# Where the last head pair's combine is traced in a hybrid decoder trunk

## The chip, the cores and the metric

The kernel runs on one core of a Trainium2 chip. The metric is the device time of one execution in microseconds (us), the median of several runs. TensorE (PE) multiplies matrices and turns blocks by multiplying with the identity; VectorE (DVE), ScalarE (ACT) and GpSimd (POOL) do elementwise work; SyncE (SP) issues the transfers between HBM and SBUF. Each engine works through its own queue in order, and semaphores tie the queues together.

## The reference

A decoder trunk of two layers over 1024 tokens of 1024 features, float32. Layer 0 has a mixer of two halves side by side; layer 1 has gated linear attention; both end in a gated feed-forward network. What matters here is layer 0's mixer, cut:

```python
def even_mixer(h, w_in, ..., w_out):
    z = h @ w_in
    u, v, q, k, vb = jnp.split(z, ...)
    a_out = chunked_gmlp(gelu(u), gelu(v), a_ln_g, a_ln_b, a_ws, a_bs)   # u * (mix of layer-normed v)
    ...
    for window, dilation in B_BRANCHES:            # ((128, 1), (512, 4), (2048, 16))
        o_r, l_r = dilated_branch(qh, kh, vh, window, dilation)
    wts = jax.nn.softmax(jnp.stack(lses), axis=0)
    o = jnp.einsum('rbhs,rbhsc->bhsc', wts, jnp.stack(outs))
    ...
    return jnp.concatenate([a_out, b_out], axis=-1) @ w_out
```

So the output projection reads, for each token, 512 features of the gMLP half (`a_out`) and 512 of the attention half (`b_out`), and `b_out` is a weighted sum of branches whose weights come from the branches' maxima and denominators.

## The kernel before, in words

Activations stand in `hq`, turned (features on partitions) and split into a high and a low fp32r part; a product is three matmuls, high by high, high by low and low by high (`PASSES`). The sequence is cut into 8 tiles of 128 tokens. One tile of a projection to 512 columns (`mm_tok`, line 190) is 8 feature blocks by 3 matmuls, 24 in all. Weights arrive raw in one of 4 buffers (`load_raw`, line 110) and are split by ACT (line 100, or 105 with a gain) and DVE (line 101, or 106) into one of `NW = 8` buffers (`wp`).

**Layer 0's mixer.** `attention` goes through four pairs of heads. `project(p)` computes q, k and v of a pair and the branch of dilation 1 into the tiles `ot{p}n0` and `ot{p}n1` (512 tokens each, with two columns for the maxima and two for the denominators); `dilated(p)` computes the other two branches together in the order of the residues and writes them to `od` in HBM (line 750). The loads `on` (line 788) bring them back in token order, in two halves `g`. `combine` and `combined` then join `ot` and `on` of half `g`: on DVE a minimum (`cM`, line 759), two subtractions (762), on ACT an `Exp` (763), on DVE two products (770), a sum (771), a reciprocal (772) and a product (773); then POOL scales the 128x512 of `ot` and DVE those of `on` (both line 776), DVE adds them (778), and SP writes the sum to `bcat[g]` (779), 128 of whose 512 columns belong to the pair.

For pairs 0 to 2 the combine is called from the next pair's `project`, behind its tiles 3 and 4 (`then`). The last pair has no next one. While its dilated branches run, `gmlp` projects v, and after each half of four tiles mixes the 8 groups (`pm`, line 605) and puts the result into `mx` (DVE, line 606). `u_proj` projects u: for each tile ACT takes the gelu (`ut`, line 616) and DVE multiplies it into `mx` (line 617). In its `consume`, behind one of the tiles, it calls `last()`, which does the last pair's combine for both halves (lines 804 to 806).

**Layer 0's output projection** (`out_first`, line 432). `prep(n)` loads `cat` (line 1122: 512 features of tile n from `bcat[n // 4]`) and `xh` (line 438), turns four blocks of `mx` and four of `cat` on PE (`pc`, line 442), and splits the result into `hq`. `AHEAD = 1`: tile 0 is prepared before the weights `wo` are split, each later tile one ahead. `out_half` multiplies (`po`, line 190), adds into `xh` (429) and writes it out (430). At tile 2 `first_sides` begins (the loads `qg`, line 219). The weights `wo` take the buffers that `wu`, the weights of u, leave. The second half's weights (`wo10r` to `wo13r`) are loaded into the raw buffers that the first half's leave.

**What sets the order.** The code is traced in program order; a planner then simulates the engines and transfers and lays each queue out anew, by program order among what it takes to be ready. `tc.keep_in_program_order` ties an instruction behind the one traced before it on its engine. The minimum `cM` is tied so; for the last pair the instruction before it is the multiply of the tile at which `last()` is called (line 617), and for the second half the last subtraction of the first. All else in the combine is placed by its data. [...] The buffers of `gv` and `ut` are the same two.

## Time and profile before

| | us |
|---|---|
| median of 3 runs | 2196.88 |
| lowest and highest | 2193.66, 2197.9 |
| the profiled execution | 2195.83 |
| its span, first to last instruction | 2194.0 |

The mean granted TensorE clock of the profiled execution is 0.994. Its span is 1.83 us shorter than its time. In what follows, a row of a timeline gives the start in us from the span's beginning, the duration in us, the engine, the line, the operation, written tile `<-` read tiles, shapes and how many instructions are merged in the row; brackets at its end give the idle time of the engine before it and what ended it. SPq is the queue of transfers issued by SyncE; a transfer's row lasts as long as its issue. The mixer of layer 0 lies in the first 400 us, the u projection between 331 and 394 us, and layer 0's output projection behind it.

### The profile page before, as it was taken

What the parts mean: (1) busy time and instruction counts of PE and PEld (TensorE: products, weight loads), DVE (VectorE), ACT (ScalarE), POOL (GpSimd) and SP (SyncE); (2) the same over time, 40 slices, a digit from 0 to 9 for tenths busy, and PEclk for the clock granted to TensorE, in tenths of its full rate; (3) what the DMA queues carried; (4) which work ended last, traced back from release to release, by engine and by line L of the source; (5) the groups of instructions that cost most, each with busy time, mean ns of one, the idle gap of its engine ahead of it and who ended that gap; (6) DMA issues with size and microseconds to landing.
All of it is one profiled execution on the core that took longest, in us unless ns stands there. A gap on an engine that the chain in (4) does not pass through costs nothing.

```text
span 2194.0 us, 29873 instructions
## 1 busy us (share of the span) xinstructions
PE 2147.0 (98%) x10508; PEld 1816.2 (83%) x10508; DVE 1533.2 (70%) x2459; ACT 1042.7 (48%) x2006; POOL 489.0 (22%) x519
## 2 busy tenths in 40 slices
PE   8999999899999999999999999999999999999999
PEld 8999987687888888878889788878788888888887
DVE  5566653567888788855577777667787878885554
ACT  6555664245444444444454455534544444454443
POOL 4444410003334342200010011110232424320000
PEclk9999999899999999999999999999999999999999
DMA  4122212565544444585563123377544454457555
GB/s 148 47 72 81 78 35 59 179 247 189 163 158 158 154 154 159 187 291 179 204 236 113 68 97 104 104 258 265 194 145 153 158 165 157 168 176 268 204 195 203
DMA packets 157254, 349.59 MB, mean 159 GB/s; under 512 B 17408, under 2 KB 54272, under 8 KB 156720
## 3 DMA queue, kind: packets, MB, share of 16 engines
q1 hardware_dynamic: 157104, 347.68, 46.9%
q8 instruction: 83, 1.36, 0.3%
q14 instruction: 67, 0.55, 0.1%
HBM read 239.02 MB, written 108.59 MB: 158 GB/s over the span
## 4 chain that ended last, share of the span: by engine, by line
PE 88%; DVE 4%; DMA 3%; ACT 3%; issue 1%; POOL 1%; SPq 0%; ACTq 0%; DVEq 0%
PE puB L290 11%; PE pgB L290 11%; PE po L190 7%; PE pj L190 6%; PE pgC L290 5%; PE puC L290 5%; PE pv L190 5%; PE pdB L397 5%; PE pdC L397 5%; PE pdO L397 4%; PE puA L290 3%; PE pgA L290 2%; PE pdP L397 2%; PE pdQ L397 2%; PE pBq L972 2%; PE pu L190 2%
## 5 line engine op out<-in xcount | busy, mean ns | idle before, releaser
L101 DVE TENSOR_TENSOR da<-ar,da 128x512 fp32r<-128x512 f32 x154 | 106.3, 690 | 156.2 <-ACT da L100 156.0
L100 ACT CAST da<-ar 128x512 fp32r<-128x512 f32 x154 | 95.9, 623 | 209.4 <-PE pdC L397 90.7
L190 PE MATMUL po<-wo,hq 128*128 128x512 f32 x768 | 186.4, 397 | 0.6 <-DVE hq L101 0.3
L190 PEld LDWEIGHTS po<-wo,hq 128*128 128x128 f32 x768 | 142.5, 189 | 30.2 <-DVE hq L101 1.4
L190 PE MATMUL pj<-wq,hq 128*128 128x384 f32 x768 | 157.8, 352 | 2.3 <-ACT vN L701 1.3
L190 PE MATMUL pv<-wv,hq 128*128 128x512 f32 (+2 forms) x768 | 141.1, 340 | 2.4 <-DVE b L1004 1.6
L190 PEld LDWEIGHTS pj<-wq,hq 128*128 128x128 f32 x768 | 135.3, 195 | 4.0 <-ACT vN L701 2.1
L397 PE MATMUL pdB<-dw,da 128*128 128x512 f32 x528 | 136.2, 391 | 0.9 <-ACT dw L100 0.9
L397 PE MATMUL pdC<-dw,da 128*128 128x512 f32 x528 | 135.8, 390 | 0.0
L190 PEld LDWEIGHTS pv<-wv,hq 128*128 128x128 f32 x768 | 118.7, 189 | 17.6 <-DVE b L1004 2.1
L397 PEld LDWEIGHTS pdB<-dw,da 128*128 128x128 f32 x528 | 98.7, 188 | 22.2 <-ACT dw L100 1.3
L397 PEld LDWEIGHTS pdC<-dw,da 128*128 128x128 f32 x528 | 99.0, 188 | 20.5
L256 POOL TENSOR_TENSOR S1g<-rg 128x512 f32<-128x512 f32 x20 | 29.3, 1464 | 384.2 <-DMA wsd<-D 325.0
L101 DVE TENSOR_TENSOR dw<-wr,dw 128x512 fp32r<-128x512 f32 x154 | 105.8, 687 | 10.7 <-ACT dw L100 10.4
L140 POOL TENSOR_SCALAR rn<-ssq 128x1 f32<-128x1 f32 x24 | 9.5, 397 | 461.3 <-ACT h L148 245.3
L397 PE MATMUL pdO<-dw,da 128*128 128x512 f32 x396 | 102.2, 389 | 0.2 <-DVE dw L101 0.2
L100 ACT CAST dw<-wr 128x512 fp32r<-128x512 f32 x154 | 95.0, 617 | 15.3 <-DMA wr<-in_w_dn 7.0
L397 PEld LDWEIGHTS pdO<-dw,da 128*128 128x128 f32 x396 | 74.3, 188 | 16.0 <-DVE dw L101 0.6
L319 DVE SCALAR_TENSOR_TENSOR t<-g,cw,t 128x1022 f32<-128x1022 f32 x44 | 75.6, 1719 | 0.1
L318 DVE SCALAR_TENSOR_TENSOR t<-g,cw,t 128x1023 f32<-128x1023 f32 x44 | 58.3, 1325 | 16.4 <-ACT t L317 16.4
L303 DVE TENSOR_TENSOR g<-g,s1g 128x512 f32<-128x512 f32 x22 | 16.2, 737 | 73.9 <-ACT s1g L302 73.9
L320 ACT ACTIVATE t<-t 128x1024 f32<-128x1024 f32 x44 | 46.7, 1061 | 29.8 <-DVE t L319 29.6
(1070 smaller groups left out, 5405.9 us busy)
## 6 DMA issues: line engine op xcount, KB each, us to landing
ar<-actd SPq DMA_DIRECT2D x70, 512.0 KB, 3.5
rd<-in_w_down SPq DMA_DIRECT2D x44, 512.0 KB, 3.6
wsd<-D SPq DMA_DIRECT2D x88, 256.0 KB, 2.6
rg<-in_w_gate SPq DMA_DIRECT2D x42, 512.0 KB, 3.6
ru<-in_w_up SPq DMA_DIRECT2D x42, 512.0 KB, 4.6
wr<-wsd SPq DMA_DIRECT2D x40, 512.0 KB, 4.5
actd<-t SPq DMA_DIRECT2D x66, 256.0 KB, 2.1
wr<-in_w_dn SPq DMA_DIRECT2D x30, 512.0 KB, 5.0
```

Source lines behind the costliest of these rows:

```text
L100: (hi or A.copy)(dst[0], src)
L101: (lo or V.tensor_sub)(dst[1], src, f32(dst[0]))
L140: G.tensor_scalar(r, ssq, 1.0 / n, EPS, op0=ALU.mult, op1=ALU.add)
L190: T.matmul(o, L[i], R[jj][:, sl], start=(k == 0 and (ii, jj) == PASSES[0]), stop=(k == nk - 1 and (ii, jj) == PASSES[-1]))
L256: G.tensor_tensor(sums[name], x, y, op=op)
L290: T.matmul(o, L[ii][:, j * P : j * P + P], right[p][:, jj, j, :], skip_group_check=more, start=(not more and j == 0 and (ii, jj) == PASSES ...
L303: V.tensor_add(C22, C22, s1)
L318: V.scalar_tensor_tensor(t[:, 1:], g[:, : S - 1], w(1), t[:, 1:], op0=ALU.mult, op1=ALU.add)
L319: V.scalar_tensor_tensor(t[:, 2:], g[:, : S - 2], w(0), t[:, 2:], op0=ALU.mult, op1=ALU.add)
L320: A.activation(t, t, AF.Silu)
L397: T.matmul(o, L[ii][:, t * P : t * P + P], R[jj], skip_group_check=more, start=start and not more and (ii, jj) == PASSES[0], stop=stop and ...
L972: T.matmul(o, L[ii][:, j * P : j * P + P], right[p][:, jj, j, :], skip_group_check=more, start=(not more and j == 0 and (ii, jj) == PASSES ...
```

## The change

In `u_proj`, `last()` is called behind the tile with index 1 instead of that with index 4. The functions that it calls are unchanged.

```diff
             A.activation(t, pj, AF.Gelu, scale=r0[:, n : n + 1])
             V.tensor_mul(mixed[n], mixed[n], t)
-            if n == 4:
+            if n == 1:
                 last()
```

What `last()` calls:

```python
def last():
    for rest in [weights(g) for g in range(2)]:   # weights(g): combine(p, g, [os[g], ons[g]])
        rest()
```

Both minima, with their subtractions and `Exp`, are traced first, then both halves of the rest.

## The prediction

> **What bounds the kernel now.** The page comes first: its span and its busy shares.

> ```profile
> span 2194.0 us, 29873 instructions
> ...
> PE 2147.0 (98%) x10508; PEld 1816.2 (83%) x10508; DVE 1533.2 (70%) x2459; ACT 1042.7 (48%) x2006; POOL 489.0 (22%) x519
> ```

> TensorE is busy for all but 47 us of the span, so an edit that takes no matmul away can gain only from those 47 us, or from matmuls that run slower than they could. The view of waits, for PE alone, says where the 47 us lie (total, times, longest):

> ```profile
> PE pc L442 <- DMA cat<-bcat: 9.3, 1, 9.3
> PE pt L529 <- DMA x<-in_x: 5.4, 2, 4.6
> ...
> PE puB L290 <- ACT s1u L302: 1.4, 2, 0.7
> ```

> The longest single wait of the whole kernel is for `cat<-bcat`, the load of what the combine of the last pair writes. The second is the start of the program, and then come waits of about one us. The tail of the u projection, from the timeline of all engines (start, duration, engine, line, tiles):

> ```profile
> 386.53 0.16 DVE L759 TENSOR_TENSOR cM<-ot3n,on 128x8 f32<-128x8 f32 x1
> ...
> 391.29 1.37 POOL L776 TENSOR_TENSOR ot3n<-ot3n,cE 128x512 f32<-128x512 f32 x1 [1.01 <-DVE cE L773]
> 391.67 1.53 DVE L778 TENSOR_TENSOR ot3n<-ot3n,on 128x512 f32<-128x512 f32 x1
> ...
> 393.23 0.36 SPq L779 DMA_DIRECT2D bcat<-ot3n  x1
> ...
> 393.56 0.60 PE L442 MATMUL pc<-ident,mx 128*128 128x128 f32 x4
> ...
> 394.10 0.69 ACT L616 ACTIVATE ut<-pu,r 128x512 f32<-128x512 f32 x1
> ...
> 394.68 0.61 ACT L100 CAST wo<-wo03r 128x512 fp32r<-128x512 f32 x1
> ...
> 396.14 0.68 DVE L778 TENSOR_TENSOR ot3n<-ot3n,on 128x512 f32<-128x512 f32 x1
> 396.74 0.68 DVE L101 TENSOR_TENSOR wo<-wo02r,wo 128x512 fp32r<-128x512 f32 x1
> 396.85 0.38 SPq L779 DMA_DIRECT2D bcat<-ot3n  x1
> ...
> 397.45 0.33 SPq L110 DMA_DIRECT2D wo12r<-in_ev_w_out  x1
> 397.82 0.47 SPq L1122 DMA_DIRECT2D cat<-bcat  x1
> ...
> 403.41 1.12 PE L442 MATMUL pc<-ident,cat 128*128 128x128 f32 x4 [9.25 <-DMA cat<-bcat]
> 404.14 1.07 ACT L100 CAST hq<-pc 128x512 fp32r<-128x512 f32 x2 [8.85 <-PE pc L442]
> ...
> 404.75 1.29 DVE L101 TENSOR_TENSOR hq<-pc,hq 128x512 fp32r<-128x512 f32 x2 [5.53 <-ACT hq L100]
> 404.77 1.22 PE L190 MATMUL po<-wo,hq 128*128 128x512 f32 x2 [0.25 <-ACT hq L100]
> ```

> The combine begins at 386.53 and its second add ends at 396.82, while PE has its last u matmul behind it at 393.56. PE turns the four `mx` blocks that it can and then stands for 9.25 us. The load it waits for was issued at 397.82, behind a weight load on the same queue, and took 5.6 us. The price is not the wait alone. The windows view (PE, PEld, DVE, ACT, POOL busy; granted clock; DMA share; GB/s) shows the clock around it:

> ```profile
> 394.20:398.00 3.80, 0.00 (x0) 0.00 (x0) 3.80 (x8) 1.09 (x2) 0.00 (x0) 0.75 0.96 261
> 398.00:403.40 5.40, 0.00 (x0) 0.00 (x0) 1.23 (x3) 0.00 (x0) 0.00 (x0) 0.50 0.97 308
> ...
> 409.00:410.00 1.00, 1.00 (x4) 0.76 (x4) 0.36 (x1) 0.59 (x1) 0.00 (x0) 0.61 0.33 115
> 410.00:411.00 1.00, 1.00 (x6) 0.82 (x5) 0.33 (x1) 0.00 (x0) 0.00 (x0) 1.00 0.85 207
> ```

> During the wait the granted clock falls to 0.50 and comes back only inside the slice 409 to 410, so the first tile of the output projection is computed at half speed. How long a tile should take is read from the starts of the transposes that open each tile's period:

> ```profile
> 413.61 0.38 PE L442 MATMUL pc<-ident,mx 128*128 128x128 f32 x2
> ...
> 420.46 0.38 PE L442 MATMUL pc<-ident,mx 128*128 128x128 f32 x2
> ...
> 426.85 0.38 PE L442 MATMUL pc<-ident,mx 128*128 128x128 f32 x2
> ```

> From 420.46 to 426.85, 6.39 us, PE does 24 `po` matmuls and 8 transposes. From 404.77 to 413.61 it does the same in 8.84 us: 2.45 us are lost to the clock.

> **The change part by part.** It takes nothing away and adds nothing. `last()` is traced after tile 1 instead of tile 4, so the pin of `cM` (L759) ties it behind the multiply of tile 1 rather than tile 4. Moved are, for two halves: 16 small DVE operations, four large DVE ones, two POOL multiplies, two `Exp` on ACT and two `bcat` writes on SP. Where they arrive, the timeline shows:

> ```profile
> 362.39 1.52 SPq L788 DMA_DIRECT2D on<-od  x2
> ...
> 367.42 1.29 DVE L617 TENSOR_TENSOR mx<-mx,ut 128x512 f32<-128x512 f32 x2
> 368.20 1.29 ACT L616 ACTIVATE ut<-pu,r 128x512 f32<-128x512 f32 x2 [8.36 <-DVE mx L617]
> 368.94 4.59 PE L190 MATMUL pu<-wu,hq 128*128 128x512 f32 x19 [0.88 <-ACT ut L616]
> ...
> 374.00 0.92 DVE L606 TENSOR_SCALAR mx<-pm,bs 128x256 f32<-128x256 f32 x2 [3.30 <-PE pm L605]
> ...
> 375.59 0.69 ACT L616 ACTIVATE ut<-pu,r 128x512 f32<-128x512 f32 x1 [6.09 <-PE pu L190]
> ...
> 378.81 1.03 PE L605 MATMUL pm<-mx,ws 128*128 128x256 f32 x4
> ...
> 382.67 1.28 ACT L763 ACT_TABLE_LOAD   x1
> ```

> The landing of `on`, from the view of that tile in this stretch, and the stretch as one window:

> ```profile
> DMA to landing us min/median/max: 3.1/3.3/3.5
> ```

> ```profile
> 368.90:386.00 17.10, 17.06 (x75) 14.20 (x76) 4.63 (x11) 3.26 (x4) 0.00 (x0) 1.00 0.00 0
> ```

> *Does it wait at its new place?* Tile 1 is projected early, but its multiply runs only at the end of the pair at 367.42, by 368.7, because it needs the first half of `mx`. The two `on` loads are issued at 362.39 and by 363.9 and take at most 3.5 us: landed by 367.4. The new wait of `cM` is 0 (bounds 0 and 1 us). Queued behind it on DVE would be the second half's evacuations (L606) and the multiplies of tiles 2 and 3.

> *DVE.* 16 small operations at 0.16 us, two multiplies and an add at 0.68, the slow add at 1.53: 2.6 + 2.0 + 1.5 = 6.1 us. In the window DVE is idle for 17.1 - 4.63 = 12.5 us, so it fits. If the whole 6.1 us stood in one block ahead of the pair at 374.00, that would end at about 376 to 377, and the next group mixing on PE, `pm` at 378.81, still finds its banks free: 0. If the block also pushes the pair that stands at 368.6, `pm` at 373 is held for up to 2 us. I take 0.

> *ACT.* Two table loads of 1.28 us and two short `Exp` go from the place at 382 to 389 to one behind the two gelus at 368.20, where ACT then sits idle for 6.09 us. Cost 0; if the planner puts them between those two gelus, the second is late by about 3 us, but PE has the 4.6 us of tile 4's matmuls at 368.94 before it needs that bank: 0 too.

> *POOL and SP.* POOL is idle in that window, SP issues nothing between 363.9 and 393.23, and the DMA share there is 0.00, so the two writes stand behind nothing. [...]

> *When the data is there.* At the old place the combine took from 386.53 to 396.82, 10.3 us with other work between. From 368.7 it ends by 379. A write and a load, each put at the 5.6 us of the slow `cat` load, bring `cat` into SBUF by 390.2, before PE asks for it at 394, with 3 to 4 us in hand. If that cover were gone, the wait would come back us for us.

> *The tail then.* PE turns eight blocks instead of four from 393.56. The first four are out at 394.16. ACT is in the last gelu until 394.79; the high part of `hq` follows, and `po` starts 0.63 us after it (404.14 to 404.77): 395.4, or 396.0 if the weight cast now at 394.68 goes first. I take 395.7. The low part on DVE (0.69) comes one step later and may hold PE for 0.4 us. The first tile then runs at full clock, 6.39 us: 395.7 + 0.4 + 6.4 = 402.5. Before, that point was 413.61. The gain is 11.1 us: 9.1 of the start, 2.4 of the clock, less 0.4.

> Bounds: if the planner turns tile 0 before the u projection ends, `po` starts near 394.0 without a wait, 413.6 - 400.4 = 13.2 us. The other end is the second layer's output projection, where both prepared tiles are turned first:

> ```profile
> 1452.22 1.03 PE L442 MATMUL pc<-ident,cat 128*128 128x128 f32 x8
> 1454.31 1.33 PE L442 MATMUL pc<-ident,cat 128*128 128x128 f32 x8 [1.06 <-DMA cat<-ogd]
> ```

> A second batch 2.1 us after the first, with its 1.3 us, puts `po` at 397.0, and with the 2 us of a held `pm` the gain is 413.6 - (397.0 + 6.4) - 2 = 8.2 us.

> A short wait on PE does not cost the clock: after the 0.88 us at 368.94 the window shows 1.00. [...]

> Sum, from the profiled execution's own 2195.83 us: 2195.83 - 11.1 = 2184.7 us. That execution lies 1.05 us below the median of the runs, so I add 0.3: 2185.0 us.

> **The rivals.**

> *A: the load stays late in its queue.* The planner issues `cat` behind the weight loads, as now at 397.82 right after `wo12r`, which waits for DVE's `wo02r` at 396.74. Without the combine's adds and multiply in DVE's queue (1.53, 0.68 and 0.68, 2.9 us at most) the load goes at 394.9 and lands 3.3 to 5.6 us later, at 398.2 to 400.5; PE still stands for 4 us or more and loses the clock. Against 403.41 the gain is 2.9 to 5.2: 2190.6 to 2192.9 us. For it: SP is one queue. Against: the weight loads wait for work that itself waits for the end of the u projection, so `cat` would be ready some 15 us earlier.

> *B: the change doesn't do what it says.* The pin sets only an earliest place; the planner may still leave the combine behind tile 4 or later. Then nothing moves: 2194 to 2198 us. Against: DVE's 12.5 us of idle time at the new place, with all inputs there.

> *C: slower.* The planner orders the whole program, and the later queues are laid out anew from shifted times. The place where that hurts is the feed-forward streams of `ffn_up`, 11 of each of two kinds in each of two layers, 44 in all: a wait such as the 0.7 us of `puB` for `s1u`, once in each stream, costs 31 us. It decides from (11.1 + 4.4) / 44 = 0.35 us per stream. From there to 0.7 us it gives 2184.7 + 15.4 to 2184.7 + 30.8, 2200 to 2215.5 us; I put it at 2204, 0.44 us per stream. For it: nothing pins that order. Against: now this wait occurs twice in 44 streams, and only one stage's arrival times change.

> **How the numbers follow.** The forecast has 0.70, with its own range 2181.5 to 2188. A has 0.10, B 0.06, C 0.14. A difference below 0.2%, 4.4 us, can't be told from none. Faster by more, below 2192.5: 0.70 and 0.07 of A, 0.77. Within: the rest of A and B, 0.09. Slower: 0.14. The range runs from 2181.5 over A and half of B to 2195; outside lie C and a few hundredths.

> **What would show it.** In the changed kernel `cM` stands at about 369, both `bcat` writes before 382, and both first `cat` loads are issued before 390. The 9.3 us row of PE's waits is gone, and the clock reads 1.00 from 394 to 411. The first `po` starts between 394 and 397.5. A `cat` issued after 395 means A; `cM` past 380 means B; PE waits that add up to more in the streams after 500 us mean C. Wrong too would be a wait of PE for `mx` L606 between 369 and 386 above 2 us.

## The result, and the profile after

| | before | after |
|---|---|---|
| median, runs side by side (4 each) | 2197.39 us | 2185.62 us |
| lowest and highest | 2193.66, 2201.47 | 2183.34, 2187.47 |
| the profiled execution, and its span | 2195.83, 2194.0 | 2186.39, 2184.3 |

The ratio is 0.995, with a 95% interval of 0.993 to 0.9969: 7 to 15 us faster, about 0.5%. The changed kernel's page, first the span, then the busy shares:

```profile
span 2184.3 us, 29872 instructions
...
PE 2143.9 (98%) x10508; PEld 1815.1 (83%) x10508; DVE 1535.4 (70%) x2459; ACT 1043.3 (48%) x2006; POOL 492.0 (23%) x519
```

The number of matmuls is the same, and PE's idle time is 2184.3 - 2143.9 = 40.4 us instead of 47.0. Its busy time fell by 3.1 us too, for the same matmuls: the windows below show the granted clock at 1.00 through the first tile, in whose first part it stood at 0.50 before. The view of waits of the changed kernel, PE alone (what it waited for: total, times, longest):

```profile
PE pt L529 <- DMA x<-in_x: 5.8, 2, 4.3
...
PE pc L442 <- DMA cat<-ogd: 2.1, 2, 1.2
```

The row of `cat<-bcat`, 9.3 us and first before, is gone; the start of the program leads. Where the combine went, in the changed kernel's timeline of all engines:

```profile
368.87 0.16 DVE L759 TENSOR_TENSOR cM<-ot3n,on 128x8 f32<-128x8 f32 x1
...
372.08 0.17 DVE L773 TENSOR_TENSOR cE<-cE,cD 128x16 f32<-128x16 f32 x1
372.33 1.55 POOL L776 TENSOR_TENSOR ot3n<-ot3n,cE 128x512 f32<-128x512 f32 x1 [33.52 <-DVE cE L773]
372.90 1.02 DVE L773 TENSOR_TENSOR cE<-cE,cD 128x16 f32<-128x16 f32 x1
...
374.05 1.50 POOL L776 TENSOR_TENSOR ot3n<-ot3n,cE 128x512 f32<-128x512 f32 x1 [0.17 <-DVE cE L773]
374.56 1.53 DVE L778 TENSOR_TENSOR ot3n<-ot3n,on 128x512 f32<-128x512 f32 x1
375.87 1.28 ACT L616 ACT_TABLE_LOAD   x1 [4.21 <-PE pu L190]
...
376.41 0.68 DVE L778 TENSOR_TENSOR ot3n<-ot3n,on 128x512 f32<-128x512 f32 x1
```

All of it stands between 368.87 and 377.1, 18 us earlier than before. The queue of SP there, from the changed kernel's timeline of that queue:

```profile
376.12 1.36 SPq L779 DMA_DIRECT2D bcat<-ot3n  x2
378.47 0.33 SPq L1122 DMA_DIRECT2D cat<-bcat  x1
378.85 0.43 SPq L438 DMA_DIRECT2D xh<-in_x  x1
379.32 0.43 SPq L1122 DMA_DIRECT2D cat<-bcat  x1
...
380.65 0.81 SPq L219 DMA_DIRECT2D qg<-in_w_gate  x2
391.36 0.33 SPq L110 DMA_DIRECT2D wo10r<-in_ev_w_out  x1
```

Both `cat` loads go right behind the writes, ahead of the weights, and with them the loads `xh` and `qg`, which stood at 398.72 and 400.15 before. The tail of the u projection and the first tile behind it, PE's timeline of the changed kernel:

```profile
393.87 0.38 PE L442 MATMUL pc<-ident,mx 128*128 128x128 f32 x2
394.08 0.38 PE L442 MATMUL pc<-ident,cat 128*128 128x128 f32 x2
...
395.80 0.73 PE L190 MATMUL po<-wo,hq 128*128 128x512 f32 x2 [0.90 <-ACT hq L100]
396.74 0.44 PE L442 MATMUL pc<-ident,mx 128*128 128x128 f32 x2 [0.20 <-DVE hq L101]
...
397.15 0.94 PE L190 MATMUL po<-wo,hq 128*128 128x512 f32 x3
...
398.27 5.06 PE L190 MATMUL po<-wo,hq 128*128 128x512 f32 x21
403.17 0.38 PE L442 MATMUL pc<-ident,mx 128*128 128x128 f32 x2
```

The clock in the same stretches, from the windows view of the changed kernel (PE, PEld, DVE, ACT, POOL busy; granted clock; DMA share; GB/s):

```profile
394.20:398.00 3.80, 2.70 (x17) 1.85 (x16) 3.02 (x5) 2.60 (x5) 0.00 (x0) 1.00 0.95 333
398.00:403.40 5.40, 5.40 (x29) 4.48 (x28) 1.87 (x3) 0.60 (x2) 0.00 (x0) 1.00 0.45 166
```

PE stands 0.90 and 0.20 us instead of 9.25 and 0.25, and the clock stays at 1.00. The gain in this stage, step by step: the first `po` starts at 395.80 instead of 404.77: 8.97 us. From there to the transposes of the next tile it is 403.17 - 395.80 = 7.37 us, with 26 `po` (2 + 3 + 21) in it against 24 before; two `po` at the rate of the last 21, (403.17 - 398.27) / 21 = 0.233 us, are 0.47, so the tile takes 6.90 instead of 8.84: 1.94 us. The u projection itself ended 0.31 us later in this execution (393.87 against 393.56). Counted from that end, the gain is 8.97 + 1.94 + 0.31 = 11.22 us; counted from the start of the span, without the 0.31, it is 10.91 us.

How much of it is kept: the first `puA` of the feed-forward network, from the timelines of PE before

```profile
518.17 1.18 PE L290 MATMUL puA<-hq,wu0p 128*128 128x512 f32 x4
```

and after

```profile
508.01 1.18 PE L290 MATMUL puA<-hq,wu0p 128*128 128x512 f32 x4
```

stands 10.16 us earlier, and the span is 9.7 us shorter: of the 10.91 us some 1.2 went back on the way, and where was not followed. In the traces, the queues of the two kernels hold their instructions in the same order outside this stage (those of DVE and PE differ between 369 and 441 us of the kernel before, SP's from the 119th to the 147th of 976 issues).

### The profile page after: what moved, and what is told of

Same layout as the page of the kernel before. It is cut to its first block, busy times and chain, and to the rows that moved or that the text cites. A ratio compares the mean times of both kernels' runs of the same rounds, so it can differ in the third digit from the quotient of the medians.

```text
span 2184.3 us, 29872 instructions
## 1 busy us (share of the span) xinstructions
PE 2143.9 (98%) x10508; PEld 1815.1 (83%) x10508; DVE 1535.4 (70%) x2459; ACT 1043.3 (48%) x2006; POOL 492.0 (23%) x519
## 4 chain that ended last, share of the span: by engine, by line
PE 84%; DMA 5%; DVE 5%; ACT 3%; issue 2%; POOL 1%; SPq 0%; ACTq 0%; DVEq 0%; POOLq 0%
PE puB L290 11%; PE pgB L290 11%; PE pgC L290 5%; PE puC L290 5%; PE pv L190 5%; PE pj L190 5%; PE pdB L397 5%; PE pdC L397 5%; PE po L190 4%; PE pdO L397 4%; PE puA L290 3%; PE pgA L290 2%; PE pdQ L397 2%; PE pdP L397 2%; PE pu L190 2%; PE pBq L972 2%
## 5 line engine op out<-in xcount | busy, mean ns | idle before, releaser
L101 DVE TENSOR_TENSOR da<-ar,da 128x512 fp32r<-128x512 f32 x154 | 106.4, 691 | 155.5 <-ACT da L100 155.3
L100 ACT CAST da<-ar 128x512 fp32r<-128x512 f32 x154 | 95.9, 623 | 207.8 <-PE pdC L397 90.7
L190 PE MATMUL po<-wo,hq 128*128 128x512 f32 x768 | 184.1, 395 | 1.3 <-ACT hq L100 0.9
L190 PEld LDWEIGHTS po<-wo,hq 128*128 128x128 f32 x768 | 141.7, 188 | 30.9 <-ACT hq L100 1.3
L190 PE MATMUL pj<-wq,hq 128*128 128x384 f32 x768 | 157.0, 351 | 2.1 <-ACT vN L701 1.1
L190 PE MATMUL pv<-wv,hq 128*128 128x512 f32 (+2 forms) x768 | 141.2, 340 | 2.4 <-DVE b L1004 1.6
L190 PEld LDWEIGHTS pj<-wq,hq 128*128 128x128 f32 x768 | 134.6, 194 | 3.8 <-ACT vN L701 1.9
L190 PEld LDWEIGHTS pv<-wv,hq 128*128 128x128 f32 x768 | 118.7, 189 | 17.6 <-DVE b L1004 2.1
L101 DVE TENSOR_TENSOR dw<-wr,dw 128x512 fp32r<-128x512 f32 x154 | 105.9, 688 | 11.2 <-ACT dw L100 10.8
L100 ACT CAST dw<-wr 128x512 fp32r<-128x512 f32 x154 | 95.0, 617 | 16.7 <-DMA wr<-in_w_dn 10.3
```

The source lines that it names most:

```text
L100: (hi or A.copy)(dst[0], src)
L101: (lo or V.tensor_sub)(dst[1], src, f32(dst[0]))
L190: T.matmul(o, L[i], R[jj][:, sl], start=(k == 0 and (ii, jj) == PASSES[0]), stop=(k == nk - 1 and (ii, jj) == PASSES[-1]))
```

## The experiments

The result agreed with the forecast, but an early combine changes several things at once: the load is early (Theory 1: the gain is the early `cat`, wait and clock together), the combine's work leaves the queues of DVE and ACT at the tail (Theory 2), and the `qg` loads come early too (Theory 3). Each kernel was timed against the kernel before on one chip. `late_load`, `warm_wait`, `first_half` and `first_half_space` stand against a median of 2196.02 us, the other four against 2193.76. The u projection ends between 390.6 and 393.9 us in the ten profiled executions, so stage times are counted from its end, the first `pc` of `mx`: before, the transposes of the next tile come 413.61 - 393.56 = 20.05 us behind it.

**The combine early, the load late.** In the changed kernel, a small write to the first `cat` tile is put at the end of DVE's queue of the u projection, so that its load has to wait for it.

```diff
-            if n == 4:
+            if n == 1:
...
-                c = pool.tile([P, 512], F32, tag="cat", name=f"cat{l}{n}")
+                c = pool.tile([P, 512], F32, tag="cat", name=f"cat{l}{n}"); n or tc.keep_in_program_order(V.memset(c[:, :1], 0.0))
```

> Combine behind tile 1 as in the changed kernel, but the buffer of the first cat load is cleared in one column by DVE, tied behind the multiply of the last u tile, so the load can't be issued before about 395.5 us. Theory 1 (the gain is the early landing of cat, and with it the clock): the wait of PE for cat comes back, 4 to 7 us of it, the clock falls to half again, the next tile's transposes start at 409 to 412 us instead of 403, and the time is 2192 to 2195 us. Theory 2 (the gain is the combine's work taken out of DVE's and ACT's queues at the tail): nothing of that comes back, 2185 to 2187 us.

Measured: 2194.47 us, ratio 0.9991 (0.9982 to 1.0). SP's queue and PE's timeline of this kernel:

```profile
374.59 1.35 SPq L779 DMA_DIRECT2D bcat<-ot3n  x2
...
393.01 1.40 SPq L1122 DMA_DIRECT2D cat<-bcat  x2
```

```profile
392.42 0.60 PE L442 MATMUL pc<-ident,mx 128*128 128x128 f32 x4
399.67 1.09 PE L442 MATMUL pc<-ident,cat 128*128 128x128 f32 x4 [6.65 <-DMA cat<-bcat]
401.00 1.22 PE L190 MATMUL po<-wo,hq 128*128 128x512 f32 x2 [0.25 <-ACT hq L100]
...
409.77 0.38 PE L442 MATMUL pc<-ident,mx 128*128 128x128 f32 x2
```

The combine is as early as in the changed kernel (`bcat` at 374.59), DVE's and ACT's queues at the tail are free of it, and still PE waits 6.65 us and needs 8.77 us for the tile. From the end of the u projection to the next transposes it is 17.35 us: 2.7 of the 11.2 us are left, and in the times 1.6 us, hardly more than none. As the explanation of the whole gain, Theory 2 falls. This kernel is also rival A, made by hand: its late load was put at a gain of 2.9 to 5.2 us, and 2.7 came.

**The clock without the wait.** In the kernel before, 38 matmuls whose result nothing reads are put ahead of the first transposes, so that PE is busy while the load is on its way.

```diff
+        d = None if l else ps.tile([P, 512], F32, tag="mm", name="dummy"); [tc.keep_in_program_order(T.matmul(d, hq[0][1][:, 0, 0, :P], hq[0][1][:, 0, 0, :], start=(i == 0), stop=(i == 37))) for i in range(0 if l else 38)]
         def prep(n):
...
```

> The kernel before, with 38 matmuls of 128x512 put on PE between the last u matmul and the first transposes of the output projection; they read hq and their result is used nowhere. They last some 8.3 us and fill most of the wait for cat. Theory 1 (the cold clock is a second price beside the wait): the load lands when it did, PE goes on at about 403.4 us, but at full clock; the first tile's 24 matmuls and 8 transposes take 6.4 to 6.9 us instead of 8.84, and the time is 2.4 us below before: 2195.0 us (2193.5 to 2196). If the clock has no price of its own: 2197.4 us, and 8.8 us for the tile.

Measured: 2194.13 us, ratio 0.9994 (0.9985 to 1.0003), which alone tells nothing apart. PE's timeline of this kernel does:

```profile
390.63 8.78 PE L434 MATMUL dummy<-hq 128*128 128x512 f32 x38
...
401.02 0.66 PE L442 MATMUL pc<-ident,cat 128*128 128x128 f32 x4 [1.17 <-DMA cat<-bcat]
402.13 0.73 PE L190 MATMUL po<-wo,hq 128*128 128x512 f32 x2 [0.46 <-ACT hq L100]
...
404.40 5.05 PE L190 MATMUL po<-wo,hq 128*128 128x512 f32 x21
409.29 0.38 PE L442 MATMUL pc<-ident,mx 128*128 128x128 f32 x2
```

The clock stays at 1.00 from 390 to 409, in the window of the first `po` too:

```profile
402.00:404.00 2.00, 1.87 (x9) 1.32 (x10) 1.29 (x2) 1.01 (x3) 0.00 (x0) 1.00 1.03 420
```

The load still comes late, but the tile takes 7.16 us with 26 `po`, so 6.69 with 24, against 8.84 in the kernel before, where the first part of it runs at 0.50. The clock's own part is 2.15 us; the other 9 of the 11.2 are the start that no longer waits.

**Half the combine early.** The changed kernel needs only `bcat[0]` for its first tiles, so the first half's combine was called behind tile 1 and the second half's left behind tile 4.

```diff
-            if n == 4:
-                last()
+            if n in (1, 4):
+                last(n)
...
-        def last():
-            for rest in [weights(g) for g in range(2)]:
-                rest()
+        def last(n):
+            g = 0 if n == 1 else 1
+            weights(g)()
```

> The combine of half 0 alone moves behind tile 1; half 1 stays behind tile 4. The first cat load reads only what half 0 writes. If the data alone holds the load back: whole gain, 2185 to 2187 us, cat issued before 390 us. If the buffer of cat lies in memory that the second half's tiles still hold (ot and on, until bcat[1] is written), the load stays behind that write: cat issued after 394 us, PE still waits 5 us or more, and the time is 2193 to 2198 us.

Measured: 2193.99 us, ratio 0.9996 (0.9987 to 1.0005). SP's queue of this kernel:

```profile
374.23 0.36 SPq L779 DMA_DIRECT2D bcat<-ot3n  x1
...
393.43 0.51 SPq L779 DMA_DIRECT2D bcat<-ot3n  x1
...
396.23 0.44 SPq L1122 DMA_DIRECT2D cat<-bcat  x1
```

The data of the first tile is written at 374.23, and its load is issued 22 us later, behind the second half's write. What it lacked was not data. The next kernel is the same, with one more edit: the `cat` buffers come from another pool, so that they lie in a place of their own.

```diff
-                c = pool.tile([P, 512], F32, tag="cat", name=f"cat{l}{n}")
+                c = small.tile([P, 512], F32, tag="cat", bufs=2, name=f"cat{l}{n}")
```

> As first_half, but the two cat buffers lie in a pool of their own that nothing used before. If memory held the load back in first_half: now the load goes behind the first bcat write at about 378 us, no wait of PE for cat, and at most 1 or 2 us of the gain are lost to half a combine at the tail: 2185 to 2188 us. If it was the second half's work on DVE that cost: no better than first_half.

Measured: 2194.46 us, ratio 0.999 (0.9981 to 0.9998). SP's queue, then PE's timeline, of this kernel:

```profile
374.44 0.36 SPq L779 DMA_DIRECT2D bcat<-ot3n  x1
376.74 0.81 SPq L1122 DMA_DIRECT2D cat<-bcat  x2
...
393.70 0.57 SPq L779 DMA_DIRECT2D bcat<-ot3n  x1
```

```profile
395.79 0.73 PE L190 MATMUL po<-wo,hq 128*128 128x512 f32 x2 [1.01 <-ACT hq L100]
398.54 0.44 PE L442 MATMUL pc<-ident,mx 128*128 128x128 f32 x2 [2.01 <-DVE hq L101]
...
406.59 0.38 PE L442 MATMUL pc<-ident,mx 128*128 128x128 f32 x2
...
473.99 2.08 PE L162 MATMUL pt<-ident,xt 128*128 128x128 f32 x12 [3.91 <-DVE xt L152]
```

With a place of its own the same load goes at 376.74, 19.5 us earlier. So in `first_half` it waited for the place. Whose memory that was no view shows; since the second half's combine is all that sets `first_half` apart from the changed kernel, it is taken to be memory that this half still held, which is argued and not shown. The time, though, was missed by 6 us and more. Two losses stand at the tail. The half combine that stays late stands in DVE's queue ahead of the split of `hq`, and PE waits 2.01 us for its low part instead of 0.20; and the clock falls, as the windows of this kernel show:

```profile
398.00:400.00 2.00, 1.46 (x9) 1.29 (x10) 1.23 (x3) 0.59 (x1) 0.00 (x0) 0.93 1.00 345
400.00:402.00 2.00, 2.00 (x8) 1.71 (x7) 1.10 (x2) 0.59 (x1) 0.00 (x0) 0.50 0.98 326
402.00:404.00 2.00, 2.00 (x8) 1.57 (x7) 0.13 (x1) 0.00 (x0) 0.00 (x0) 0.72 1.05 419
```

The next transposes come 406.59 - 393.75 = 12.8 us behind the end of the u projection, against 9.3 in the changed kernel, for the same 26 `po`: 1.8 us more of wait, and about 1.7 us, an estimate, half of the 3.4 us for which these windows put the clock at 0.50. Further on, 3.91 us go at 473.99, where the loads `xt` came late, and the clock falls for another 3.4 us, by the windows, behind that wait (0.98 from 470 to 475, 0.68 from 475 to 480). This profiled execution, 2198.08 us, is the slowest of the kernel's eleven, so its losses add up to more than the median's. Why the loads came late was not settled: the issue of the first at 463.00 comes 6.5 us after the queue's issue before it, and a place in memory that comes free later is only a guess. Theory 2, with little effect where the load is late, has its share where the load is early: a half combine left at the tail gives back 3.5 of the 11.2 us there.

**Own place alone.** The changed kernel with that one edit, which parts the two reasons.

> The changed kernel with the two cat buffers in the pool of their own, as in first_half_space; the queues stay the same but for the place of one xh load. If first_half_space lost its gain through where the buffers lie: a loss here too, 0.997 to 0.999 of before. If through the late second half (half a combine in DVE's queue at the tail, and the buffers of the next stage still held): 0.994 to 0.996, as the changed kernel.

Measured: 2185.12 us, ratio 0.9964 (0.9949 to 0.9978), as the changed kernel. Its waits for `xt` are 1.6 us in all, 1.1 at the first. So the loss of `first_half_space` comes with the half combine left late.

**Other tiles.** `last()` behind tile 3, still ahead of the mixing of the second half, and behind tile 7, the last.

```diff
-            if n == 4:
+            if n == 3:
```

> The combine behind tile 3 instead of tile 1. Theory 1 (any place before the second half's mixing is as good): cM at about 371 us, both bcat writes before 381, cat issued before 384, no wait of PE for cat; the first po between 395 and 397 us and the time that of the changed kernel, 0.994 to 0.997 of before. Rival (the place itself decides, each tile later costs some): between the changed kernel and before, 0.997 to 0.999.

```diff
-            if n == 4:
+            if n == 7:
```

> The combine behind the last tile. Theory 1 (the tail is as long as the combine is late): cM at about 395.5 us, bcat written at 400 to 403, cat issued at about 405 and landed at 408 to 411, PE waits 15 us, and the time is 5 to 8 us above before: 1.002 to 1.004. Rival (from tile 4 on it makes no difference, since the weight loads fill the queue anyway): 1.000.

Measured: 2186.08 us, ratio 0.9966 (0.9955 to 0.9977), for tile 3, and 2199.5 us, 1.0024 (1.0013 to 1.0035), for tile 7. PE's timeline and SP's queue of the kernel with tile 7:

```profile
404.66 1.11 PE L442 MATMUL pc<-ident,cat 128*128 128x128 f32 x4 [12.24 <-DMA cat<-bcat]
```

```profile
399.56 0.98 SPq L779 DMA_DIRECT2D bcat<-ot3n  x2
401.93 0.33 SPq L1122 DMA_DIRECT2D cat<-bcat  x1
```

Tile 3 is as good a place as tile 1, both ahead of the second half's mixing (tile 3's combine starts at 369.6, with the first `cat` load at 377.39). Behind the mixing, time is lost as the load gets later: 9.25 us of wait at tile 4, 12.24 at tile 7 (15 were expected; the planner lets the weights pass, so the load isn't held by them).

**The `qg` loads.** In the changed kernel, the two `qg` loads are held until behind the fourth `cat` load; the other queues and SP's own order beside them stay.

```diff
-                Q.dma_start(c, rows(bcat[n // 4], n % 4))
+                cats.append(Q.dma_start(c, rows(bcat[n // 4], n % 4)).ins)
...
-                Q.dma_start(r, w_of(kind)[l, i])
+                with tc.issue_after(cats[3]) if l == 0 and kind == "g" else ExitStack(): Q.dma_start(r, w_of(kind)[l, i])
```

> The changed kernel with the two loads qg of the gate weights' first tiles issued behind the fourth cat load, at about 399 us as before the change, instead of at 381; every queue but SP's is the same. Theory 3 (a part of the gain stays only because these loads, whose buffers lie where the combine's tiles lay, come early too): the tail of the u projection is unchanged, but the work on the sides and then the first tiles of the second half are late, PE waits 3 to 5 us at about 465 us, and the time is 0.997 to 0.999 of before. If only the cat load matters: 0.994 to 0.996, with no wait of PE above 1 us between 410 and 500 us.

Measured: 2185.61 us, ratio 0.9958 (0.9946 to 0.9971). The loads go at 397.39 instead of 380.65, and the time loses nothing, though PE waits up to 1.6 us for `xt` where less than 1 was expected. Theory 3 falls. What is left is Theory 1, the early load, with its condition from Theory 2: DVE free of the combine at the tail, where half a combine gave back 3.5 us. Not tried: the 0.90 and 0.20 us of wait that remain at the tail.

## Why the prediction was right, step by step

The forecast was 2185.0 us and the median 2185.62; the sum for the profiled execution was 2184.7 and its time 2186.39. The path was right, from the early combine over the early load to the wait and the clock. That the median came within 0.6 us is in part luck: the four runs of the changed kernel alone lie 4 us apart, and the interval of the gain is 7 to 15 us.

- *The place of the combine.* `cM` stands at 368.87 as said (about 369), without a wait for `on`. The writes were said to come before 382 and the first two `cat` loads before 390: 376.12 and 378.47.
- *DVE and ACT.* Costed at nothing, rightly: the u projection ended 0.31 us later, and 0.24 of that stood at the eight `pm` ahead of the combine already (366.00 against 365.76). The slow rows came: the second product took 1.02 us instead of 0.17 while POOL multiplied, an add 1.53 instead of 0.68. Both overlap POOL's multiplies (1.55 us from 372.33, 1.50 from 374.05), as the add of 391.67 did before; the add at 376.41, with POOL done, took 0.68, but DVE's multiply at 373.95 took only 0.69 beside POOL too. What makes the slow rows slow was not shown. PE waited nowhere for `mx` L606. The gelu's table load at 375.87 falls into a time when ACT sat idle.
- *When the data is there.* The cover was underrated. The loads of `cat` took at most 5.1 us from issue to landing, so the first was there by 383.6, more than 10 us before PE turns it at 394.08, where 3 to 4 us were counted on.
- *The tail.* `po` was put at 395.4 or, if the weight cast goes first, 396.0. The cast did go first (at 394.65), and `po` starts at 395.80. The low part cost 0.20 us instead of 0.4.
- *The clock.* Right in kind, wrong in size. The step took 6.39 us for a tile at full clock, from a tile in the middle of the stream, and so 2.45 us for the clock. With the clock held up, `warm_wait` shows 6.69 us and the changed kernel 6.90 - 0.20 = 6.70: the first tile runs dry once, its first two `po` taking 0.73 us instead of 2 x 0.233, so the clock's share is 2.15 us. In the forecast's own count, from the start of the span, the gain is 8.97 + 2.15 - 0.20 = 10.9 us where 11.1 was said: the misses of the clock and of the low part nearly cancel, which is luck too. That a short wait costs no clock, read off one wait of 0.88 us, was too wide a rule: in `first_half_space` waits of 1.01 and 2.01 us were followed by some 3.4 us at 0.50. When the clock fell and came back in the traces is told in the last section; what decides it was not shown.
- *The rivals.* A didn't come, since the planner put the loads ahead of the weights; `late_load` shows what it would have cost: 2.7 us of gain left. B didn't come. C didn't: the later queues are in the same order, and `puB` waits 1.4 us for `s1u` in all, as before.

What the prediction left out: that the `xh` and `qg` loads, traced behind `cat`, move with it (no cost, by `qg_late`), and that the load waits for a place as well as for data. Had only half the combine been moved, the same reasoning would have forecast most of the gain, and `first_half` shows none. Nor did the forecast see that the combine's work on DVE costs PE time at the tail once the load is early.

## What to carry to other kernels

A long wait of PE at the seam of two stages is priced as wait plus the slow matmuls behind it (here 9.25 us and 2.15 us), and it is removed by moving the whole chain that ends in the awaited load into a stretch where the engines of that chain are idle (here DVE was for 12.5 of 17.1 us). When a load is issued long after its data was written (22 us in `first_half`), look for the tiles whose memory its buffer takes: it may be they that have to be finished first. Once the load lands before it is needed, an earlier place brings nothing more: the ratio is 0.9966 behind tile 3 and 0.995 behind tile 1, with intervals that overlap.

## What the runs showed of the hardware

```profile
392.72:396.13 3.41, 1.44 (x9) 0.99 (x7) 3.41 (x6) 2.44 (x5) 0.00 (x0) 1.00 0.58 154
...
402.96:406.37 3.41, 2.71 (x9) 1.97 (x10) 1.29 (x2) 1.07 (x2) 0.00 (x0) 0.50 1.03 372
406.37:409.79 3.42, 3.42 (x13) 2.83 (x12) 0.85 (x2) 1.17 (x2) 0.00 (x0) 0.50 0.86 346
409.79:413.20 3.41, 3.41 (x17) 2.78 (x16) 0.54 (x1) 0.00 (x0) 0.00 (x0) 1.00 0.30 77
```

Three things were measured at this seam, in the busy share of PE in such slices. At the fall, the slice ahead of 0.50 had a share of 0.42 or less (0.42 here; an estimate of 0.41 in `first_half_space`, where 1.01 and 2.01 us of wait stand close together; 0.39, 0.24 and 0.11 in `first_half`, `late_load` and `tile7`, all from PE's timelines and the stretches above); behind 0.74, in the changed kernel with its 0.90 and 0.20 us (392.95 to 396.37), the clock stayed at 1.00, as it did in `warm_wait` with waits of 1.17 and 0.46 us. Elsewhere in the same traces, shares between these went either way (0.56 at 334.93 in the changed kernel was followed by 0.50, 0.53 at 1198.50 was not), so no threshold was shown. At the return, 0.79 (402.96 here) was followed by another slice at 0.50, and 1.00 (406.37 here) and 0.93 (`tile7`, an estimate made the same way) by 1.00; elsewhere in the changed kernel 0.95 at 143.78 was not enough and 0.84 at 338.34 was. And the time from the restart of PE to full clock was 6.4 us before the change, 6.2 in `late_load`, 4.7 in `first_half` and 4.4 in `tile7`: in these four, counted in slices back from the return, PE restarted within one slice, and 1.00 came at the end of the next. What sets the slices was not shown.
